# The forget gate's sigmoid written as exponential, addition and reciprocal

## The chip, the cores and the metric

One core of a Trainium2 chip runs the whole program. The metric is device time in microseconds; lower is better. A core has five engines with queues of their own: PE (TensorE, matmuls), DVE (VectorE), ACT (ScalarE, tables of functions), POOL (GpSimd) and SP (here it issues the transfers). Each queue is worked off in order, and the queues meet at semaphores only.

## What is computed

One layer of a hybrid encoder on 1024 positions of 1024 channels: four token mixers (gated recurrence, pooling, sparse attention with a top-k, attention into memory), gates, an output projection and a SwiGLU feed-forward part. The change lies in the gated recurrence (HGRN2), in four heads of 128 channels:

```python
sg = jax.nn.sigmoid(f_logit.astype(F32))
f = lbf + (1.0 - lbf) * sg
log_f = jnp.log(jnp.maximum(f, LOG_FLOOR))
k = (1.0 - lbf) * (1.0 - sg)
...
b = jnp.cumsum(lfc, axis=1)
o_inter = jnp.einsum('bthk,bhkv->bthv', qc * jnp.exp(b), S)
...
att = jnp.einsum('bthk,bshk,btshk->bhts', qc, kc, decay)
```

The sparse attention that runs beside it finds the 256th largest score of each row and masks the keys below it:

```python
top_val, top_idx = lax.top_k(score, n_sel)
```

## The kernel before

Everything is computed in transposed form, channels on the 128 partitions, in two halves of 512 positions. Each fp32 operand of a matmul is split into a high part (ACT copies it, rounded) and a low part (DVE subtracts), and a product takes three matmuls: lines 302 to 304 for a unit, where a unit is a block of 128 columns of weights times 8 blocks of channels. `Unit.split` (L283, L284) writes the tiles `wh` and `wl`, of which there are three each, and `run` splits three units ahead. The result of a unit lies in PSUM (`psB`, two buffers) until its `evac` has read it.

Beside this main line run generators, one step or so per unit: `hgrn_gen` (the recurrence of one head), `topk_gen` (a search for the threshold, bit by bit, ACT counts at L704 and DVE decides at L757 and L759; `finish`, L706 to L730, then builds the mask `bias`, of which POOL does the last step at L727 and which goes through DRAM as `bid`), `dsa_gen` (attention: scores plus bias on DVE at L804, Exp on ACT at L811 to `P`, transposes on PE at L821, copy to `PT`, product with the values at L828) and `mem_gen`. Up to the feed-forward part, a planner fills each engine's queue from the order in which the program writes the work and from when it expects operands to be ready, so neighbours in a queue need not be neighbours in the program.

The forget gate of one head and one half is `ev_hf` (L930 to L944). It reads the logits from PSUM (`p`) and works in slots of the tile `hw` (128x8x512): slot 0 is `k`, slot 4 `sg` (later f), slot 5 `fb` (later a scaled copy of f for the logarithm). Sigmoid on ACT at L934, then six TENSOR_SCALARs on DVE, L936 to L942. The unit of the query follows (`ev_hq`, a Tanh at L175), then `hgrn_gen`: two Ln on ACT (L959, L960), their sum (L961), a cumulative sum (L964), seven levels of differences, exponentials and products (L978 to L986) and small gram products on PE (L997, L1015, L1033). Slots 4 to 6 of `hw` serve as work space there; the last reader of slot 5 is L1027. `ev_hf` is called eight times: four heads in each half.

Of the kernel before, what the change touches and what calls it, by code (L numbers as in the profile page):

```python
# [15 lines left out]
AF = mybir.ActivationFunctionType  # L16
OP = mybir.AluOpType
# [19 lines left out]
def tile_hybrid_block(ctx, tc, x, x_t, mem_t, cols, w_in, w_gate, w_branch, w_out, hgrn_norm,  # L37
                      pool_w, w_mem_kv, norm_mix_post, norm_ffn_pre, norm_ffn_post,
                      w_ffn_gate_up, w_ffn_down, out):
    nc = tc.nc  # L40
# [203 lines left out]
    def need(e):  # L244
        if e in side:
            for _ in e[0]:
                pass
            side.remove(e)
# [681 lines left out]
    def ev_hf(h, hd):  # L930
        def f(p):
            need(S.get(("hgrn", h, hd - 1)))
            k, sg, fb = S["hw"][:, 0, :], S["hw"][:, 4, :], S["hw"][:, 5, :]
            nc.scalar.activation(sg, p, AF.Sigmoid)  # L934
            lb, om = lbt[:, hd, 0:1], lbt[:, hd, 1:2]
            nc.vector.tensor_scalar(k, sg, -1.0, 1.0, op0=OP.mult, op1=OP.add)  # L936
            nc.vector.tensor_scalar(k, k, om, 0.5, op0=OP.mult, op1=OP.mult)
            nc.vector.tensor_scalar(sg, sg, om, lb, op0=OP.mult, op1=OP.add)
            big = 2.0 ** 40
            nc.vector.tensor_scalar(fb, sg, big, float(np.float32(1e-30)) * big, op0=OP.mult, op1=OP.max)  # L940
            nc.vector.tensor_scalar(fb, fb, 1.0, None, op0=OP.min)
            nc.vector.tensor_scalar(sg, sg, 1.0 / big, None, op0=OP.max)  # L942
            S["hf"] = (sg, fb)
        return f  # L944
# [723 lines left out]
```

## Time and profile before

| | us |
|---|---|
| median of 3 runs | 1768.8 (1763.12 to 1772.54) |
| the profiled execution, its own time | 1767.2 |
| its span, first to last instruction | 1765.5 |
| PE busy | 1709.4 |
| DVE busy | 1199.8 |
| ACT busy | 896.5 |
| mean granted clock of TensorE | 0.985 |

PE is busy nearly all the time, and its busy time counts matmuls in flight. So an engine's own total says little; the question is at which places PE had to wait, and for whom. The profile names for each idle stretch the instruction that ended it, the releaser. The granted clock is given as a share of the full 2.4 GHz.

### The profile page before, as it was taken

What the parts mean: (1) busy time and instruction counts of PE and PEld (TensorE: products, weight loads), DVE (VectorE), ACT (ScalarE), POOL (GpSimd) and SP (SyncE); (2) the same over time, 40 slices, a digit from 0 to 9 for tenths busy, and PEclk for the clock granted to TensorE, in tenths of its full rate; (3) what the DMA queues carried; (4) which work ended last, traced back from release to release, by engine and by line L of the source; (5) the groups of instructions that cost most, each with busy time, mean ns of one, the idle gap of its engine ahead of it and who ended that gap; (6) DMA issues with size and microseconds to landing.
All of it is one profiled execution on the core that took longest, in us unless ns stands there. A gap on an engine that the chain in (4) does not pass through costs nothing.

```text
span 1765.5 us, 26374 instructions
## 1 busy us (share of the span) xinstructions
PE 1709.4 (97%) x9776; PEld 1421.4 (81%) x9776; DVE 1199.8 (68%) x2459; ACT 896.5 (51%) x1623; POOL 237.4 (13%) x261
## 2 busy tenths in 40 slices
PE   6999989999999999999999998899999999999997
PEld 5888867888887877888788887788888888888886
DVE  6587898777696579678666558687777777532533
ACT  5469867757656768776443343333223323422421
POOL 1020000000000010000000001332332231221321
PEclk8999999999999999999999999999999999999999
DMA  6756232222333573223242243323222321743534
GB/s 176 205 181 173 57 131 82 76 85 70 108 108 111 199 239 92 68 61 91 64 144 86 85 129 122 87 87 94 80 78 83 91 78 52 277 150 124 173 114 167
DMA packets 231296, 206.46 MB, mean 117 GB/s; under 512 B 16896, under 2 KB 194176, under 8 KB 230784
## 3 DMA queue, kind: packets, MB, share of 16 engines
q1 hardware_dynamic: 231168, 204.78, 37.5%
q8 instruction: 77, 1.26, 0.3%
q14 instruction: 51, 0.42, 0.1%
HBM read 167.26 MB, written 33.29 MB: 114 GB/s over the span
## 4 chain that ended last, share of the span: by engine, by line
PE 77%; DVE 11%; ACT 5%; DMA 3%; issue 3%; POOL 1%; SPq 0%; DVEq 0%; ACTq 0%; POOLq 0%
PE psB L302 8%; PE psB L304 8%; PE psB L303 8%; PE psA L1326 5%; PE psA L1327 5%; PE psA L1325 4%; PE psB L1325 2%; PE psB L1327 2%; PE psB L1326 2%; PE psA L1472 2%; PE psA L1471 2%; PE psA L1470 2%; DVE wl L284 2%; ACT cjunk L704 2%; PE psC L303 2%
## 5 line engine op out<-in xcount | busy, mean ns | idle before, releaser
L302 PE MATMUL psB<-uTh,wh 128*128 128x512 f32 x800 | 322.1, 403 | 1.5 <-ACT sig L1148 1.0
L304 PE MATMUL psB<-uTh,wl 128*128 128x512 f32 x800 | 315.4, 394 | 0.5 <-DVE wl L284 0.5
L303 PE MATMUL psB<-uTl,wh 128*128 128x512 f32 x800 | 315.6, 395 | 0.0
L284 DVE TENSOR_TENSOR wl<-raw,wh 128x1024 fp32r<-128x1024 f32 (+3 forms) x138 | 157.1, 1141 | 119.7 <-ACT wh L283 119.2
L283 ACT ACTIVATE wh<-raw 128x1024 fp32r<-128x1024 f32 (+3 forms) x138 | 136.0, 989 | 147.7 <-PE psB L303 112.1
L304 PEld LDWEIGHTS psB<-uTh,wl 128*128 128x128 f32 x800 | 151.7, 190 | 33.7 <-DVE wl L284 1.0
L302 PEld LDWEIGHTS psB<-uTh,wh 128*128 128x128 f32 x800 | 151.9, 190 | 33.0 <-ACT sig L1148 1.3
L303 PEld LDWEIGHTS psB<-uTl,wh 128*128 128x128 f32 x800 | 152.2, 190 | 29.8
L1220 DVE TENSOR_TENSOR hx<-hr,hx 128x1024 fp32r<-128x1024 f32 x44 | 78.1, 1810 | 95.5 <-ACT hx L167 95.4
L704 ACT ACTIVATE cjunk<-scr,cst 128x640 bf16<-128x640 f32 (+3 forms) x124 | 122.2, 985 | 40.5 <-DVE cst L759 35.4
L1342 ACT ACTIVATE th<-hid 128x512 f32<-128x512 f32 x44 | 27.8, 632 | 132.5 <-DVE hid L1217 132.5
L167 ACT ACTIVATE wh<-raw 128x1024 fp32r<-128x1024 f32 x22 | 23.3, 1060 | 116.0 <-issue 95.1
L1220 POOL TENSOR_TENSOR wl<-raw,wh 128x1024 fp32r<-128x1024 f32 x22 | 55.9, 2541 | 183.1 <-ACT wh L167 182.9
L180 POOL TENSOR_TENSOR rstd<-ms,mhalf 128x1 f32<-128x1 f32 (+2 forms) x35 | 26.9, 771 | 390.4 <-DVE ms L196 219.0
L1326 PE MATMUL psA<-xc,wcwl 128*128 128x512 f32 x176 | 69.5, 395 | 3.6 <-DVE xc L171 3.6
L1325 PE MATMUL psA<-xc,wcwh 128*128 128x512 f32 x176 | 69.8, 396 | 0.0
L1325 PE MATMUL psA<-xc,wcwl 128*128 128x512 f32 x176 | 69.7, 396 | 0.0
L1327 PE MATMUL psA<-xc,wcwl 128*128 128x512 f32 x176 | 69.5, 395 | 0.0
L1327 PE MATMUL psA<-xc,wcwh 128*128 128x512 f32 x176 | 69.3, 393 | 0.0
L1326 PE MATMUL psA<-xc,wcwh 128*128 128x512 f32 x176 | 69.0, 392 | 0.0
L1470 PE MATMUL psA<-wh,hx 128*128 128x512 f32 x176 | 68.5, 389 | 0.0
L1472 PE MATMUL psA<-wh,hx 128*128 128x512 f32 x176 | 68.5, 389 | 0.0
(501 smaller groups left out, 4301.0 us busy)
## 6 DMA issues: line engine op xcount, KB each, us to landing
raw<-in_w_gate_dram SPq DMA_DIRECT2D x64, 512.0 KB, 3.7
hr<-hidd SPq DMA_DIRECT2D x44, 512.0 KB, 6.0
raw<-in_w_in_dram SPq DMA_DIRECT2D x36, 512.0 KB, 4.0
raw<-in_w_ffn_gate_up_dram SPq DMA_DIRECT2D x22, 512.0 KB, 4.2
rawu<-in_w_ffn_gate_up_dram SPq DMA_DIRECT2D x22, 512.0 KB, 5.4
hidd<-hid SPq DMA_DIRECT2D x44, 256.0 KB, 2.2
raw<-in_w_ffn_down_dram SPq DMA_DIRECT2D x22, 512.0 KB, 4.5
praw<-in_w_branch_dram SPq DMA_DIRECT2D x64, 128.0 KB, 3.1
```

The costliest lines, as they stand in the source:

```text
L283: nc.scalar.activation(self.hi[:, r], self.raw[:, r], AF.Copy)
L284: nc.vector.tensor_tensor(self.lo[:, r], self.raw[:, r], f32(self.hi[:, r]), op=OP.subtract)
L302: nc.tensor.matmul(p[:, ns], whi[:, k, :], xh[:, k, ns], start=(k == 0), stop=False)
L303: nc.tensor.matmul(p[:, ns], whi[:, k, :], xl[:, k, ns], start=False, stop=False)
L304: nc.tensor.matmul(p[:, ns], wlo[:, k, :], xh[:, k, ns], start=False, stop=(k == nk - 1))
L704: nc.scalar.activation(junk[:, 0:e.L], e.sc, AF.Sign, bias=bias, accum_out=e.sum)
L1220: (eng or nc.vector).tensor_tensor(o, a, b, op=OP.subtract)
L1325: nc.tensor.matmul(p, wh[:, k], xh[:, k], start=k == 0, stop=False)
L1326: nc.tensor.matmul(p, wh[:, k], xl[:, k], start=False, stop=False)
L1327: nc.tensor.matmul(p, wl[:, k], xh[:, k], start=False, stop=k == 3)
L1470: nc.tensor.matmul(acc, self.xh[:, a, ts_], self.wh[:, a], start=f, stop=False)
L1472: nc.tensor.matmul(acc, self.xl[:, a, ts_], self.wh[:, a], start=False, stop=e)
```

## The change

The Sigmoid activation becomes an Exp of the negated logits into slot 5 of `hw`, an addition of one in place, and a reciprocal from slot 5 into slot 4. The rest of `ev_hf` stays.

```diff
             k, sg, fb = S["hw"][:, 0, :], S["hw"][:, 4, :], S["hw"][:, 5, :]
-            nc.scalar.activation(sg, p, AF.Sigmoid)
+            nc.scalar.activation(fb, p, AF.Exp, scale=-1.0)
+            nc.vector.tensor_scalar(fb, fb, 1.0, None, op0=OP.add)
+            nc.vector.reciprocal(sg, fb)
             lb, om = lbt[:, hd, 0:1], lbt[:, hd, 1:2]
             nc.vector.tensor_scalar(k, sg, -1.0, 1.0, op0=OP.mult, op1=OP.add)
```

## Rows read from the trace of the kernel before

**Rows 1.** The page's first part: busy us, share and instructions of each engine.

```profile
PE 1709.4 (97%) x9776; PEld 1421.4 (81%) x9776; DVE 1199.8 (68%) x2459; ACT 896.5 (51%) x1623; POOL 237.4 (13%) x261
```

**Rows 2.** Stretches: us, each engine's busy us (instructions), clock, DMA share, GB/s.

```profile
250.00:400.00 150.00, 145.95 (x1124) 121.36 (x1124) 116.36 (x333) 105.81 (x202) 7.38 (x7) 0.97 0.27 79
```

**Rows 3.** PE's waits, 250 to 1000 us (total, times, longest), and ACT's group L283.

```profile
PE psA L828 <- ACT PT L167: 3.6, 3, 2.2
PE psA L821 <- ACT P L811: 2.7, 2, 2.4
...
L283 ACT ACTIVATE wh<-raw 128x1024 fp32r<-128x1024 f32 (+3 forms) x138 | 136.0, 989 | 147.7 <-PE psB L303 112.1
```

**Rows 4.** Groups of instructions on ACT: busy us, mean ns, idle before.

```profile
L934 ACT ACT_TABLE_LOAD x8 | 10.3, 1283 | 0.1
```

**Rows 5.** Timeline of ACT, four places: start us, us, line, operation.

```profile
252.02 1.28 ACT L934 ACT_TABLE_LOAD   x1
253.32 0.60 ACT L934 ACTIVATE hw<-psB 128x512 f32<-128x512 f32 x1
...
259.69 1.28 ACT L811 ACT_TABLE_LOAD   x1 [2.04 <-DVE mx L809]
...
272.36 0.60 ACT L811 ACTIVATE P<-P,mx 128x384 f32<-128x384 f32 x1
...
274.08 0.57 ACT L1148 ACTIVATE sig<-psB 128x512 f32<-128x512 f32 x1
...
737.42 1.28 ACT L811 ACT_TABLE_LOAD   x1
```

**Rows 6.** Groups of instructions on DVE, forms apart: busy us, mean ns.

```profile
L941 DVE TENSOR_SCALAR hw<-hw 128x512 f32<-128x512 f32 x8 | 3.4, 425 | 0.1
...
L830 DVE RECIPROCAL rc<-sm 128x1 f32<-128x1 f32 x16 | 2.5, 159 | 5.4 <-ACT P L811 5.4
...
L887 DVE RECIPROCAL rcs<-sums 128x4 f32<-128x4 f32 x8 | 1.4, 173 | 2.8 <-ACT P L870 2.8
L185 DVE TENSOR_SCALAR ms<-hss 128x4 f32<-128x4 f32 x8 | 1.3, 165 | 0.1
...
L185 DVE TENSOR_SCALAR ms<-ss 128x1 f32<-128x1 f32 x8 | 1.2, 150 | 2.8 <-ACT un L201 2.8
```

**Rows 7.** Timeline of DVE and PE, the first gate's first gram operands and products.

```profile
280.40 0.42 DVE L986 TENSOR_TENSOR hw<-hw 128x256 f32<-128x256 f32 x1
...
284.63 1.36 PE L997 MATMUL psA<-hw 128*32 128x32 f32 x128
```

**Rows 8.** Timeline of DVE and PE at the seventh gate and after it.

```profile
819.38 0.42 DVE L1068 TENSOR_TENSOR hw<-psA,rstd 128x256 f32<-128x256 f32 x1 [0.90 <-POOL rstd L180]
...
837.72 0.69 DVE L804 CUSTOM_DVE_ANT_0 P<-psA,bias 128x512 f32<-128x512 f32 x1 [1.26 <-DMA bias<-bid]
...
841.28 1.19 PE L821 MATMUL psA<-ident,P 128*128 128x128 f32 x8 [2.38 <-ACT P L811]
```

**Rows 9.** Timeline of POOL, DVE and PE after the first gate.

```profile
265.72 1.49 POOL L727 TENSOR_SCALAR sc<-sc 128x512 f32<-128x512 f32 x1 [8.85 <-DVE sc L726]
...
268.26 0.55 DVE L804 CUSTOM_DVE_ANT_0 P<-psA,sc 128x384 f32<-128x384 f32 x1
...
272.51 1.15 PE L821 MATMUL psA<-ident,P 128*128 128x128 f32 x6 [0.28 <-ACT P L811]
```

**Rows 10.** The fifth gate: two stretches of 10 us, and timeline of DVE and PE.

```profile
660.00:670.00 10.00, 7.73 (x33) 6.30 (x32) 9.64 (x26) 6.66 (x12) 3.02 (x1) 0.73 0.42 134
...
670.00:680.00 10.00, 10.00 (x46) 8.21 (x45) 8.63 (x16) 9.21 (x14) 0.00 (x0) 0.93 0.17 52
...
664.07 0.44 DVE L936 TENSOR_SCALAR hw<-hw 128x512 f32<-128x512 f32 x1
...
691.28 0.42 DVE L986 TENSOR_TENSOR hw<-hw 128x256 f32<-128x256 f32 x1
...
691.42 0.66 PE L997 MATMUL psA<-hw 128*32 128x32 f32 x54
```

## The prediction

> **What bounds the kernel now.** I read the page's busy lines first: PE has a matmul in flight for 97% of the span, DVE is busy 68%, ACT 51% [rows 1]. So a change on ACT and DVE moves the end only where PE waits for it, or where a wait lets the granted clock fall. Then the stretches: the forget gate runs eight times (four heads, two halves of the sequence), between 252 us and 906 us. From 250 to 400 us, where the first two of them run, PE is idle for 150.00 - 145.95 = 4.05 us while DVE stands at 116.36 of 150.00, or 78% [rows 2]. The list of PE's waits over the whole zone is short; its two largest entries, 3.6 and 2.7 us, are on work of the sparse attention (P and PT), none on the forget gate itself [rows 3]. The split of the weights has its own cover: ACT's copy to wh sat idle 147.7 us, of which 112.1 until PE had left the old buffer [rows 3], so those buffers are refilled the moment they are free, about two units of matmuls before they are read. A few us more on DVE don't reach PE by that way.
>
> What can reach PE is a chain that passes through DVE where DVE has no room. I call the eight gates 1 to 8 in order of time.
>
> **What goes: table loads on ACT.** Before each Sigmoid stands an ACT_TABLE_LOAD: eight of 1283 ns [rows 4]. Exp and Tanh don't force loads on each other (the Exp at 272.36 us and the Tanh at 274.08 us have none between them) [rows 5], so an Exp in the Sigmoid's place needs none. At gates 1, 2, 5 and 6 the next function after the Sigmoid, Tanh apart, is an Exp of the attention, which pays a load only because the Sigmoid's table came in between (four loads, the first at 259.69 us, the last at 737.42 us) [rows 5]. The loads for Ln, and those for the function after it, stay. So 12 loads go: 12 x 1.28 = 15.4 us of ACT. What are they worth? One load takes 252.02 to 253.30 us, and the ACTIVATE starts 0.02 us later [rows 5]. The Trainium skill ("ScalarE: Activation LUTs", section What ACT_TABLE_LOAD costs) puts a switch at about 2.66 us, with a drain of 1.38 us; the trace does not show that drain, and by the page the loads would come to 32 us of ACT, still off PE's path. I book 0 as the value: none of PE's waits above has a vanishing load as its last releaser. The cover is PE's own queue; without it a gate would gain at most 1.3 us. The Exp itself costs what the Sigmoid did (0.60 us), and it releases the PSUM bank up to 1.3 us earlier.
>
> One wait is new: Exp writes slot 5 of hw, which L940 on DVE wrote first before. Its last reader of the gate before is L1027, in a step that the code forces to be issued before the next gate begins (the call of need at L932), and DVE reaches it long before PE has finished the unit of the next gate. Cost 0; were it late, the copies to wh would stand behind it on ACT, and they have two units of lead.
>
> **What comes: two DVE instructions per gate.** The addition in place has the form of L941 (128x512 in SBUF, immediate operands): 425 ns [rows 6]. The reciprocal of 128x512 is nowhere in the trace; the ones there have 1 to 4 elements per partition. Lower bound: another one-source DVE pass over the same tile, 0.42 us. Upper bound from its own rows: 159 ns at one element, 173 ns at four, so 4.7 ns each, times 512, plus 0.15: 2.5 us. Plain TENSOR_SCALAR grows from 150 to 165 ns over the same step, so these rows don't settle the slope [rows 6]. I take 2.5 us, since it is worked out from the only rows of this operation, and keep 0.42 for the range. So a gate adds 0.43 + 2.5 = 2.9 us to DVE (0.85 at the lower bound), eight gates 23.4 us.
>
> The Trainium skill ("VectorE: DVE Perf Modes", section First, the fixed hardware budget) describes the reciprocal as an iterative divide with a repeat count of 8. Read as eight passes per element it would, as an estimate with that page's 0.96 GHz, give 4.3 us, and by it the sum below would be 5.4 us higher; from one to four elements it would add 25 ns where the rows add 14 ns, so the trace speaks rather against that reading.
>
> **What lies on PE's path.** Inside a gate the chain gets 2.9 us of DVE and loses 1.3 us of ACT: +1.6 us until the first gram product on PE. At gate 1 the last operand is ready at 280.40 + 0.42 = 280.82 us and PE comes at 284.63 us, 3.8 us later [rows 7]; that is the least of all gates but the fifth. So the gate's own chain costs 0 outside gate 5. What remains is what the 2.9 us push back on DVE's queue, at three places.
>
> Gate 7: the same DVE queue holds the end of the last top-k row, whose bias goes from DVE over POOL to DRAM and back; L804 waits 1.26 us for that DMA at 837.72 us, and PE waits 2.38 us for its P at 841.28 us [rows 8]. There is no slack behind DVE here. Ahead of it, among the gate's own steps, DVE has a gap of 0.90 us [rows 8] that takes up part. So 2.9 - 0.9 = +2.0 us.
>
> Gate 1: the bias of a row leaves POOL at 265.72 + 1.49 = 267.21 us and the P that needs it starts at 268.26 us, so 1.0 us is free; PE then waits for that P already, 0.28 us at 272.51 us [rows 9]. So 2.9 - 1.0 = +1.9 us.
>
> Gate 5: DVE is busy 9.64 of 10 us, and the granted clock is 0.73 there [rows 10], since PE has just waited 2.2 us for PT (the longest of [rows 3]). The gate's first DVE step, L936, only starts at 664.07 us [rows 10], behind the work on which that wait hangs; in its place the new two come too late to lengthen it. But its gram has no slack: the last operand is written from 691.28 us on and PE begins at 691.42 us [rows 10]. The gaps of DVE on the way take up some, 10 - 8.63 = 1.4 us from 670 to 680 us [rows 10]. So 2.9 - 1.4 = +1.5 us.
>
> Gates 2, 3, 4, 6 and 8: no PE wait for DVE within reach, 0. Together 2.0 + 1.9 + 1.5 = +5.4 us: the profiled execution of 1767.2 us (span 1765.5 us and 1.7 us around it) would become 1772.6 us. It lies 1.6 us under the median of 1768.8 us, so against the median the forecast is **1774 us**.
>
> **Rivals.** (a) DVE turns into the bound at gates 1, 5 and 7, slower: all three pass on the full 2.9 us (8.7 us), and one more stretch runs at a clock as in 660 to 670 us, which costs (1 - 0.73) x 10 = 2.7 us. That gives 1768.8 + 11.4 = 1780 us. It decides from the point at which the gaps that I counted (0.9, 1.0 and 1.4 us) are already spoken for, or the new pair is put ahead of the top-k work. For it: DVE is at 96% from 660 to 670 us [rows 10]. Against: a gate's steps may be queued late, as L936 was. (b) The reciprocal is a plain pass at the lower bound, 0.42 us: the pair is then 0.85 us and fits in each of the gaps; 1768.8 us, no change. For it: the plain rows grow by as much as the reciprocal's [rows 6]. (c) ACT is what PE waits for: if the loads saved shorten the longest waits for PT and P (2.2 and 2.4 us) and give back one slow-clock stretch (2.7 us), 1768.8 - 7.3 = 1761 us. Against: these waits hang on DVE and a DMA. (d) The change doesn't do what it says: the queues are filled by a planner, which may put Exp and Ln so that loads come back or other work is reordered. I see no sign in the rows; within some us of no change.
>
> **How the numbers follow.** The forecast gets 0.50, (a) 0.25, (b) 0.14, (c) 0.05, (d) 0.06. The range goes from (c), 1761, to a little over (a), 1784, since the runs before lie within 1763.12 to 1772.54 us and the pair could add a further stretch at low clock. About 0.5%, or 8.8 us, is what a measurement can tell from no change. Forecast, (b) and (d) fall within; (a) lies above; half of (c) and a small part of (d) lie below 1760. Hence faster 0.03, same 0.71, slower 0.26.
>
> **What would show it.** Right: no Sigmoid load, 12 loads fewer, an ACT total some 15 us lower; a reciprocal row of about 2.5 us and DVE up by about 23 us; the PE wait of 2.38 us at gate 7 longer by some 2 us; the end within 10 us. Wrong: a reciprocal over 3 us with several PE waits for DVE (then a), under 0.7 us (then b), or PE waits that shrink after gates 2 and 6 (then c). A changed order of work far from the gates would make the whole sum void.

## The result and the profile after

The changed kernel takes 1776.4 us (median of 7 runs, 1773.4 to 1777.5), the kernel before 1764.8 us (7 runs, 1760.9 to 1772.5). The measured ratio of the two is 1.0051, with a 95% interval of 1.0034 to 1.0067. A repeat, among the experiments below, gave 1.0063 (1.0050 to 1.0075). So the change costs some 9 to 11 us. The forecast was 1774 us within 1761 to 1784 us, from a kernel before of 1768.8 us, the median of its first three runs; so the change itself was forecast at 5.4 us. The profiled execution of after took 1777.5 us (span 1775.8 us), against 1767.2 us (span 1765.5 us) before: 10.3 us between these two traces.

The busy time of each engine, from the page of after, answers to [rows 1]:

```profile
PE 1711.4 (96%) x9776; PEld 1420.6 (80%) x9776; DVE 1225.2 (69%) x2475; ACT 875.5 (49%) x1607; POOL 236.7 (13%) x261
```

ACT has 21.0 us less than before, DVE 25.4 us more. PE has the same number of instructions; it is idle for 64.4 us instead of 56.1 us and busy for 2.0 us longer. So most of the 10 us are idle time of PE, and the rest goes with stretches at a lower clock, as at gate 5 below. Next, the groups of instructions of after, on DVE and then on ACT (busy us, mean ns, idle time before); they answer to [rows 4, 6]:

```profile
L936 DVE RECIPROCAL hw<-hw 128x512 f32<-128x512 f32 x8 | 26.8, 3348 | 0.1
L935 DVE TENSOR_SCALAR hw<-hw 128x512 f32<-128x512 f32 x8 | 3.4, 424 | 0.1
...
L962 ACT ACT_TABLE_LOAD x8 | 10.3, 1283 | 0.1
L1150 ACT ACT_TABLE_LOAD x6 | 7.7, 1283 | 0.1
L811 ACT ACT_TABLE_LOAD x3 | 3.8, 1283 | 0.1
L961 ACT ACT_TABLE_LOAD x3 | 3.8, 1283 | 0.1
L870 ACT ACT_TABLE_LOAD x2 | 2.6, 1283 | 0.0
...
```

Line numbers behind L934 are two higher than before. The reciprocal takes 3348 ns, eight times a plain pass and above the upper bound of 2.5 us. No load stands on L934 any more; 23 loads are left of 39.

Where PE waits, 245 to 1170 us of after (us in total, times, longest us); this answers to [rows 3]:

```profile
PE psC L302 <- ACT ymb L167: 6.3, 2, 4.2
PE psA L821 <- ACT P L811: 5.0, 3, 2.4
...
PE psB L302 <- DVE hw L176: 3.2, 2, 2.5
...
PE psA L828 <- ACT PT L167: 1.5, 2, 1.3
```

Two entries stand out: ymb, the operand of the pooling mixer's projection, and `hw` at L176, the Tanh step of the query. The kernel before has one wait for ymb, of 2.1 us, at another place, which stays; the one of 4.2 us is new, and so are both waits for L176 (2.53 us, and 0.62 us behind gate 7). None of them was in the forecast.

To see where the time is lost I cut each trace at PE's own marks: the score product (L802) near 248 us, then the first gram product after gates 1, 2, 3, 4, 5 and 8, then the end. Each number below is the difference of two starts on PE's timeline, in us, from one profiled execution of each kernel. What each kernel does is told with the experiments.

| kernel | to gate 1 | 1 to 2 | 2 to 3 | 3 to 4 | 4 to 5 | 5 to 8 | 8 to the end |
|---|---|---|---|---|---|---|---|
| before | 35.7 | 59.4 | 87.6 | 65.6 | 194.2 | 238.2 | 835.9 |
| after | 37.4 | 59.7 | 88.9 | 65.6 | 199.2 | 239.9 | 837.2 |
| after, again | 36.2 | 59.7 | 90.5 | 65.5 | 199.2 | 240.4 | 838.9 |
| cheap instruction for the reciprocal | 31.6 | 59.3 | 87.5 | 65.6 | 195.5 | 237.8 | 838.3 |
| Tanh, not folded | 32.5 | 59.4 | 87.6 | 65.5 | 195.3 | 236.1 | 837.3 |
| Tanh folded in | 31.4 | 59.4 | 87.3 | 65.5 | 195.3 | 238.9 | 837.5 |
| half a reciprocal | 34.7 | 59.3 | 89.0 | 65.5 | 197.6 | 237.2 | 839.0 |
| reciprocal in four pieces | 37.2 | 59.4 | 87.6 | 65.5 | 199.3 | 238.1 | 837.6 |
| reciprocal twice | 40.4 | 59.7 | 87.9 | 65.6 | 206.0 | 238.5 | 836.6 |
| Sigmoid kept, reciprocal behind it | 38.8 | 59.3 | 92.8 | 65.5 | 200.8 | 240.1 | 837.4 |
| new form at gates 1 to 4 | 37.2 | 59.7 | 88.9 | 65.6 | 195.3 | 235.3 | 836.5 |
| new form at gate 5 alone | 35.5 | 59.3 | 87.3 | 65.6 | 199.1 | 239.6 | 838.0 |
| new form at gates 6 to 8 | 35.5 | 59.3 | 87.7 | 65.6 | 195.2 | 240.3 | 837.3 |
| new form but at gate 5 | 37.4 | 59.7 | 89.0 | 65.5 | 195.3 | 240.7 | 837.6 |

Between before and after: +1.7 at gate 1, +0.3, +1.3 at gate 3, 0, +5.0 at gate 5, +1.7 from 5 to 8 and +1.3 behind, together 11.3 us; after reaches the first mark 1.0 us earlier (247.98 against 248.95 us), so 10.3 us remain, as between the spans. The start of the first mark differs by up to 6 us between these executions (244.8 to 251.1 us), and the last column scatters from 835.9 to 839.0 us without a pattern; neither is read as an effect. A difference of 1 us in one row is not read either, unless other rows repeat it: after and its repeat are the same kernel, with DVE's steps in the same order, and differ by 1.2 us up to gate 1 and by 1.6 us from gate 2 to 3. Beside the kernel before (194.2 us from gate 4 to 5), six other kernels without a reciprocal at gate 5 take 195.2 to 195.5 us there, so that of the +5.0 us some 3.7 to 4.0 us are left against those.

**Gate 5, the largest part.** The timeline of after, DVE, then ACT, then PE (start us, us, engine, line; in brackets the idle time before and its releaser):

```profile
668.66 3.34 DVE L936 RECIPROCAL hw<-hw 128x512 f32<-128x512 f32 x1
...
672.38 0.22 DVE L759 SCALAR_TENSOR_TENSOR cst<-cst,cbits 128x1 int32<-128x1 int32 x1
...
675.79 0.75 DVE L1131 TENSOR_SCALAR ypb<-psA,colt 128x512 f32<-128x512 f32 x1
...
672.69 1.15 ACT L704 ACTIVATE cjunk<-scr,cst 128x1024 bf16<-128x1024 f32 x1 [4.19 <-DVE cst L759]
...
673.84 1.04 ACT L283 ACTIVATE wh<-raw 128x1024 fp32r<-128x1024 f32 x1
674.90 1.28 ACT L962 ACT_TABLE_LOAD   x1
...
676.73 0.62 ACT L167 ACTIVATE ymb<-ypb 128x512 fp32r<-128x512 f32 x1
...
677.39 0.80 PE L302 MATMUL psC<-ymb,pjw 128*128 128x512 f32 x1 [4.24 <-ACT ymb L167]
```

Read it from the end. PE stands 4.24 us at the head of its queue for ymb. ACT writes ymb at 676.73 us, from ypb, which DVE writes at 675.79 us. DVE comes to it late: the reciprocal holds it from 668.66 to 672.00 us, and 16 steps of the gate itself, the search and the sparse attention stand between it and ypb. ACT too stands still, 4.19 us, for the threshold's next step (L759 at 672.38 us), so its own queue, with the weights' copy and the Ln's load ahead of ymb, starts late. The same place in the kernel before, DVE, ACT and PE:

```profile
670.10 0.75 DVE L1129 TENSOR_SCALAR ypb<-psA,colt 128x512 f32<-128x512 f32 x1 [0.33 <-PE psA L1127]
...
673.24 0.61 ACT L167 ACTIVATE ymb<-ypb 128x512 fp32r<-128x512 f32 x1
...
664.59 2.80 PE L828 MATMUL psA<-svt,PT 128*128 128x64 f32 x12 [2.23 <-ACT PT L167]
```

There DVE still waited for PE before ypb, and PE did not wait for ymb. Its 2.23 us for PT are gone in after, which waits 1.66 us for P instead, ahead of the reciprocal, at 663.05 us. Between the marks of gates 4 and 5 PE is idle for 194.2 - 189.3 = 4.9 us before and for 199.2 - 189.0 = 10.2 us after; that is all of the +5.0. Two stretches of after show it (us, busy us of PE, PEld, DVE, ACT, POOL, granted clock, DMA share, GB/s), beside [rows 10]:

```profile
670.00:680.00 10.00, 4.75 (x17) 3.11 (x17) 10.00 (x25) 7.23 (x10) 0.00 (x0) 0.85 0.14 41
680.00:690.00 10.00, 9.51 (x39) 7.37 (x38) 7.93 (x18) 6.42 (x11) 0.00 (x0) 0.81 0.19 52
```

DVE is busy in the whole of the first one while PE works less than half of it; the granted clock then falls below its full level, as it did after the PT wait in the kernel before.

**Gate 1 and gate 3**, one line of before, then the timeline of after:

```profile
262.25 0.67 DVE L176 SCALAR_TENSOR_TENSOR hw<-hw,psB 128x512 f32<-128x512 f32 x1
```

```profile
258.03 3.35 DVE L936 RECIPROCAL hw<-hw 128x512 f32<-128x512 f32 x1
...
267.37 0.69 DVE L176 SCALAR_TENSOR_TENSOR hw<-hw,psB 128x512 f32<-128x512 f32 x1
...
268.11 0.79 PE L302 MATMUL psB<-uTh,wh 128*128 128x512 f32 x1 [2.53 <-DVE hw L176]
...
415.01 0.39 PE L863 MATMUL psA<-mkt,mqs 64*128 64x256 f32 x1 [1.07 <-ACT PT L167]
```

At gate 1 DVE's step L176 is the last reader of a `psB` buffer. It stands behind the gate's own steps and ran at 262.25 us before; now it runs at 267.37 us, and the unit that needs the buffer waits 2.53 us (3.56 us in the repeat).

### The profile page after: what moved, and what is told of

It reads as the page before. It is cut to its first block, busy times and chain, and to the rows that moved or that the text cites. A ratio compares the mean times of both kernels' runs of the same rounds, so it can differ in the third digit from the quotient of the medians.

```text
span 1775.8 us, 26367 instructions
## 1 busy us (share of the span) xinstructions
PE 1711.4 (96%) x9776; PEld 1420.6 (80%) x9776; DVE 1225.2 (69%) x2475; ACT 875.5 (49%) x1607; POOL 236.7 (13%) x261
## 4 chain that ended last, share of the span: by engine, by line
PE 52%; DVE 5%; ACT 2%; DMA 1%; issue 1%; POOL 1%; DVEq 0%; POOLq 0%; SPq 0%; ACTq 0%
PE psA L1328 5%; PE psA L1329 5%; PE psA L1327 4%; PE psB L302 3%; PE psB L304 3%; PE psB L303 3%; PE psB L1327 2%; PE psB L1329 2%; PE psB L1328 2%; PE psA L1473 2%; PE psA L1472 2%; PE psA L1474 2%; PE psC L1329 1%; PE psC L1328 1%; PE psC L1327 1%; PE psC L1473 1%
## 5 line engine op out<-in xcount | busy, mean ns | idle before, releaser
L283 ACT ACTIVATE wh<-raw 128x1024 fp32r<-128x1024 f32 (+3 forms) x138 | 136.1, 990 | 173.8 <-PE psB L303 134.8
L1222 POOL TENSOR_TENSOR wl<-raw,wh 128x1024 fp32r<-128x1024 f32 x22 | 56.1, 2551 | 182.9 <-ACT wh L167 182.7
```

The source lines that it names most:

```text
L283: nc.scalar.activation(self.hi[:, r], self.raw[:, r], AF.Copy)
L1222: (eng or nc.vector).tensor_tensor(o, a, b, op=OP.subtract)
```

## The experiments

**The theory** after the result: the cost is DVE's, the 3.35 us of one reciprocal at the head of a queue that serves other engines. **The rivals**: the planner's other order of work (rival B in the expectations where it is named), and the loads, which might be worth something after all. All edits are against the changed kernel unless said; ratios are against the kernel before, on the same chip.

**A cheap instruction in the reciprocal's place.**

```diff
-            nc.vector.reciprocal(sg, fb)
+            nc.vector.tensor_scalar(sg, fb, 0.25, 1.0, op0=OP.mult, op1=OP.min)
```

> Exp and addition as in the changed kernel, but in the reciprocal's place one TENSOR_SCALAR of the same tile (times 0.25, at most 1), so the division is left out. Theory A (the 3.35 us of each reciprocal at the head of DVE's queue is the loss): DVE falls by about 8 x 2.9 = 23 us, the PE waits of 4.24 us (gate 5) and 2.53 us (gate 1) go, ratio to the kernel before 0.998 to 1.001. Rival B (the planner's other order of work is the loss, whatever the new instructions last): ratio still about 1.005. Rival C (the loads saved on ACT are worth time by themselves): ratio under 0.997, since some 20 us of table loads are gone at nearly no price on DVE.

Measured: 1766.6 us against 1766.5 us, ratio 1.0002 (0.9991 to 1.0012). The page of this kernel:

```profile
PE 1707.0 (97%) x9776; PEld 1416.7 (80%) x9776; DVE 1202.9 (68%) x2475; ACT 880.9 (50%) x1611; POOL 237.0 (13%) x261
```

27 loads are left, exactly 12 fewer than before, and ACT has 15.6 us less. With the same number of new steps, the same Exp and the same new wait, nothing is lost. Is the other order of the work the cause, then? The planner makes another order of this kernel than of after in many places (27 loads against 23). But around the two gates where after waits most, DVE's queue holds the same steps in the same order in both: from 246 to 276 us of after, at gate 1, and from 507 to 701 us, at gate 5; ACT has one step at another place in each. Gate 5 with the cheap instruction, on DVE:

```profile
664.40 0.41 DVE L936 TENSOR_SCALAR hw<-hw 128x512 f32<-128x512 f32 x1
...
665.20 0.21 DVE L759 SCALAR_TENSOR_TENSOR cst<-cst,cbits 128x1 int32<-128x1 int32 x1
...
668.60 0.75 DVE L1131 TENSOR_SCALAR ypb<-psA,colt 128x512 f32<-128x512 f32 x1
```

The step at L936 takes 0.41 us instead of 3.34 us, ypb starts 4.2 us behind it instead of 7.1 us, and PE's wait for ymb is 1.14 us instead of 4.24 us; the wait at gate 1 is 0.78 us instead of 2.53 us (lines further below). At these two gates the order is thus not the cause. At the other gates it differs, and this run does not tell the two apart. Nothing is gained in the total by the loads either. At gate 1 they are worth something, though: 31.6 us instead of 35.7 up to its gram. PE's waits of the kernel before for sig (1.0 us) and for P ([rows 9]) are not there, and its granted clock from 270 to 280 us is 1.00 instead of 0.83. The kernels with Tanh have 31.4 and 32.5 us, those with a Sigmoid at gate 1 35.5 to 35.7 us. Whether it is the loads themselves or the order that comes with their absence was not told apart. Where these 3 to 4 us go in the total is not settled: it is not in one later stretch.

**The Sigmoid kept, with the addition and the reciprocal behind it.**

```diff
-            nc.scalar.activation(fb, p, AF.Exp, scale=-1.0)
+            nc.scalar.activation(fb, p, AF.Sigmoid)
```

> Sigmoid kept on ACT with its table loads, but written where the Exp writes and followed by the same addition and reciprocal (so the gate's value is 1/(1+sigmoid), not the reference's). Theory A: the DVE part is the loss and the loads are worth nothing, so the ratio stays at 1.004 to 1.007. Rival C: the loads saved gave back part of it, so without that saving the ratio goes to 1.008 or more (20 us of ACT more, of which a third would reach PE).

Measured: 1780.4 us, ratio 1.0081 (1.0067 to 1.0095), above both ratios of after and where rival C was expected. So beside the reciprocal the loads seem to cost 0.2 to 0.3% (3 to 5 us), though without it their absence shows no gain in the total; against the repeat of after the two intervals overlap. PE's waits of this kernel from 245 to 1000 us, then a wait at gate 3:

```profile
PE psA L821 <- ACT P L811: 10.8, 3, 6.3
...
414.28 0.38 PE L863 MATMUL psA<-mkt,mqs 64*128 64x256 f32 x1 [1.81 <-ACT PT L167]
```

At gate 5 PE now waits 6.3 us for P instead of 4.2 us for ymb. The stretch from gate 2 to 3 takes 92.8 us (88.9 and 90.5 in after), that from 4 to 5 200.8 us (199.2 in both).

**Sigmoid by Tanh, without a reciprocal** (against the kernel before).

```diff
-            nc.scalar.activation(sg, p, AF.Sigmoid)
+            nc.scalar.activation(sg, p, AF.Tanh, scale=0.5)
+            nc.vector.tensor_scalar(sg, sg, 0.5, 0.5, op0=OP.mult, op1=OP.add)
```

> Only the half of the change that removes the table loads: the sigmoid as 0.5 tanh(x/2) + 0.5, Tanh on ACT in place of Exp, and one TENSOR_SCALAR on DVE in place of addition and reciprocal. Theory A: DVE gets 8 x 0.42 = 3.4 us, ACT loses some 15 to 20 us of loads; nothing of this lies on PE's path, ratio 0.998 to 1.001. Rival B: any new instruction reorders the work, ratio anywhere from 0.995 to 1.006 without a cause in the gate. Rival C: 0.997 or less.

Measured: 1763.7 us, ratio 0.9989 (0.9977 to 1.0002), 27 loads, DVE 1200.7 us. Not told apart from the kernel before.

**The reciprocal in four pieces.**

```diff
-            nc.vector.reciprocal(sg, fb)
+            for c in range(4):
+                s = slice(c * 128, (c + 1) * 128)
+                nc.vector.reciprocal(sg[:, s], fb[:, s])
```

> The changed kernel with the reciprocal cut into four instructions of 128 columns, so that other work of DVE can go between them; DVE's total is the same or some 0.4 us per gate more. Theory A in its strict form (the block of 3.35 us at the queue's head is what hurts, not the total): the ratio falls to 1.000 to 1.003. If the total of DVE's work near the gates is what hurts: ratio stays at 1.004 to 1.007. Four instructions of about 0.9 us each are expected.

Measured: 1772.3 us, ratio 1.0034 (1.0021 to 1.0046). The reciprocal's line in this kernel (ns least, median, largest; first and last start), then PE's waits:

```profile
L938 DVE RECIPROCAL hw<-hw x32: 892/896/955, 254.9 to 911.0; 128x128 f32<-128x128 f32 x32
...
PE psC L302 <- ACT ymb L167: 6.3, 2, 4.2
```

The total on DVE is no smaller (4 x 896 = 3584 ns), the wait for ymb is the same 4.2 us and from gate 4 to 5 it takes 199.3 us. What came back is at gate 3 (87.6 us instead of 88.9 and 90.5) and from 5 to 8 (238.1 instead of 239.9 and 240.4). But it did not come back because other steps went in between: at gates 3, 4, 5, 6 and 8 the four pieces follow each other without a gap, and only at gates 1, 2 and 7 do other steps stand among them. Two whole reciprocals give nearly the same two rows (87.9 and 238.5 us, below). So this run does not test whether the block or the total hurts, and its ratio, which lies between the two expectations and overlaps that of after, stays unexplained.

**Half of the reciprocal** (the other 256 columns get a cheap instruction).

```diff
-            nc.vector.reciprocal(sg, fb)
+            nc.vector.reciprocal(sg[:, 0:256], fb[:, 0:256])
+            nc.vector.tensor_scalar(sg[:, 256:512], fb[:, 256:512], 0.25, 1.0, op0=OP.mult, op1=OP.min)
```

> The changed kernel with a reciprocal of 256 columns and a TENSOR_SCALAR on the other 256 (there the division is left out). The reciprocal should last 1.7 to 1.8 us. Theory A: half the dose, ratio 1.001 to 1.003, under half of the whole one's 1.0051 if gaps of DVE take up the first microsecond. A threshold only (nothing until the gaps are full): 1.000.

**The reciprocal twice** (the second one's result is not read).

```diff
             nc.vector.reciprocal(sg, fb)
+            nc.vector.reciprocal(fb, fb)
```

> The changed kernel with a second reciprocal behind the first at every gate (on the slot that is overwritten later; the result is the reference's). DVE gets 8 x 3.35 = 26.8 us more. Theory A (DVE's queue near the gates, with part of each 3.35 us passed on to PE): the second dose costs more than the first, since the gaps are used up: ratio 1.010 to 1.016. If the planner hides what it knows of: 1.005 to 1.008.

Measured: half of it takes 1750 ns and gives 1770.1 us, ratio 1.0032 (1.0016 to 1.0047); two give 1783.7 us, ratio 1.0100 (1.0085 to 1.0115). PE's waits at gate 1 and gate 5, first with the cheap instruction alone, then half, then twice (one fence for each kernel):

```profile
268.30 0.50 PE L302 MATMUL psB<-uTh,wh 128*128 128x512 f32 x1 [0.78 <-DVE hw L176]
...
670.06 0.73 PE L302 MATMUL psC<-ymb,pjw 128*128 128x512 f32 x2 [1.14 <-ACT ymb L167]
```

```profile
264.76 0.50 PE L302 MATMUL psB<-uTh,wh 128*128 128x512 f32 x1 [2.32 <-DVE hw L176]
...
671.76 0.72 PE L302 MATMUL psC<-ymb,pjw 128*128 128x512 f32 x2 [3.38 <-ACT ymb L167]
```

```profile
268.11 0.79 PE L302 MATMUL psB<-uTh,wh 128*128 128x512 f32 x1 [5.95 <-DVE hw L176]
...
683.01 0.80 PE L302 MATMUL psC<-ymb,pjw 128*128 128x512 f32 x1 [7.27 <-ACT ymb L167]
```

And the stretch of the last kernel in which its longest wait ends (columns as above):

```profile
680.00:690.00 10.00, 6.13 (x16) 4.56 (x17) 8.14 (x20) 7.60 (x10) 0.00 (x0) 0.50 0.17 52
```

With 0, 256, 512 and twice 512 columns of reciprocal at each gate the wait at gate 5 is 1.14, 3.38, 4.24 (4.22 in the repeat) and 7.27 us, the one at gate 1 0.78, 2.32, 2.53 (3.56) and 5.95 us, and the ratio 1.0002, 1.0032, 1.0051 to 1.0063, and 1.0100. Up to gate 1's gram it takes 31.6, 34.7, 36.2 to 37.4, and 40.4 us, from gate 4 to 5 195.5, 197.6, 199.2 and 206.0 us. From one reciprocal to two the wait at gate 5 grows by 3.03 us and the one at gate 1 by 2.4 to 3.4 us, nearly its whole 3.35 us. Of the 6.8 us at gate 5, 3.0 us are idle time of PE and 3.9 us longer busy time (192.9 against 189.0 us), which goes with the clock: in the last line it is 0.50, the lower of its two levels (1.2 GHz) for the whole stretch. Two of the expectations failed: half the columns cost half of the loss or more, not less, and the second reciprocal adds 0.0037 to 0.0049, no more than the first. No size shows below which the reciprocal would be free.

**Which gates.** `ev_hf` with the new form at some gates and the Sigmoid at the others:

```diff
-            nc.scalar.activation(fb, p, AF.Exp, scale=-1.0)
-            nc.vector.tensor_scalar(fb, fb, 1.0, None, op0=OP.add)
-            nc.vector.reciprocal(sg, fb)
+            if (h, hd) == (1, 0):
+                nc.scalar.activation(sg, p, AF.Sigmoid)
+            else:
+                nc.scalar.activation(fb, p, AF.Exp, scale=-1.0)
+                nc.vector.tensor_scalar(fb, fb, 1.0, None, op0=OP.add)
+                nc.vector.reciprocal(sg, fb)
```

This one keeps the Sigmoid at gate 5. The others turn the condition round (new form at gate 5 alone), or use `h == 0` (new form at gates 1 to 4) or `h == 1 and hd > 0` (gates 6 to 8) for the new form.

> The changed kernel, but the fifth gate alone keeps its Sigmoid. By the traces the distance between the two kernels grows by 6 us of 9 around the fifth gate, where DVE has no gap. If that is so, this gives back 4 to 7 us: ratio 1.001 to 1.003. If the loss belongs to all gates alike (1.1 us each): 1.0045. If the planner's order moves the loss elsewhere: 1.004 or more with the wait of 4.24 us at another place.

> The new form at gate 5 alone, Sigmoid at the other seven. If the block of 3.35 us in DVE's full queue at gate 5 is the main place: a PE wait for ymb of about 4 us there, ratio 1.002 to 1.004. If a single gate is never worth more than its share: 1.0006, not to be told from 1.

> The new form at gates 1 to 4 (first half of the sequence), Sigmoid at the others. By the traces the changed kernel is 2.4 us behind when gate 5 begins, of which 1.7 us from gate 1. If the loss sits where the traces show it: ratio 1.001 to 1.002. If it belongs to all gates alike: 1.0025 to 1.003.

> The new form at gates 6 to 8, Sigmoid at the others. By the traces the distance grows by some 1 to 2 us from gate 6 to the end, and gate 7, where 2.0 us was forecast, shows none: ratio 1.000 to 1.001. If the forecast for gate 7 holds after all: 1.001 to 1.002. If all gates are alike: 1.002.

> The changed kernel once more, unedited, on the chip and beside the runs of the three kernels below, so that the parts can be set against the whole. Ratio 1.0034 to 1.0067, as before.

| new form at gates | us | ratio | 95% |
|---|---|---|---|
| 1 to 4 | 1767.4 | 1.0000 | 0.9988 to 1.0013 |
| 5 | 1772.7 | 1.0031 | 1.0020 to 1.0042 |
| 6 to 8 | 1768.2 | 1.0005 | 0.9994 to 1.0016 |
| all but 5 | 1774.2 | 1.0046 | 1.0034 to 1.0059 |
| all (after, again) | 1778.9 | 1.0063 | 1.0050 to 1.0075 |

PE's wait at gate 5 in the kernel that has the new form there alone:

```profile
672.24 0.79 PE L302 MATMUL psC<-ymb,pjw 128*128 128x512 f32 x1 [4.20 <-ACT ymb L167]
```

Gate 5 alone makes the ymb wait of after, the stretch of 199.1 us, and, on its own, about half of the loss (0.0031 of 0.0051 to 0.0063). In the kernel without it there the ymb wait is absent and PE's 2.1 us for PT are back. But taken out of the eight it gives back only 0.0005 to 0.0017, where 1.001 to 1.003 was expected for the rest. The parts don't add up: 0.0000 + 0.0031 + 0.0005 = 0.0036 against 0.0063 (each with an interval of about 0.0012 to either side, so this difference is barely clear of noise), and all gates but 5 cost 0.0046 where the two groups alone give 0.0005 (this one is clear of it). The table of marks shows where: with the new form at gates 1 to 4 the loss there is the full 1.5 + 0.3 + 1.3 us, and the stretch from 5 to 8, which has the Sigmoid as before, is 2.9 us shorter (235.3 against 238.2). With one plain reciprocal at gates 6 to 8 that stretch takes 239.9 to 240.7 us, without one 235.3 to 239.6 us, and with two 238.5 us; so no price of these three gates can be read from it. The planner makes another order out of each kernel; which step of that order saves the 2.9 us was not found, and why they are not there in the kernel with all gates stays open.

**Tanh with its halves folded into the constants**, so that nothing is added on DVE (against the kernel before).

```diff
-    lbt = st([128, 4, 2], name="lbt")
+    lbt = st([128, 4, 4], name="lbt")
...
+        nc.vector.tensor_scalar(lbt[:, :, 2], lbt[:, :, 1], 0.5, None, op0=OP.mult)
+        nc.vector.tensor_tensor(lbt[:, :, 3], lbt[:, :, 0], lbt[:, :, 2], op=OP.add)
...
-            nc.scalar.activation(sg, p, AF.Sigmoid)
-            lb, om = lbt[:, hd, 0:1], lbt[:, hd, 1:2]
+            nc.scalar.activation(sg, p, AF.Tanh, scale=0.5)
+            omh, lbh = lbt[:, hd, 2:3], lbt[:, hd, 3:4]
...
-            nc.vector.tensor_scalar(k, k, om, 0.5, op0=OP.mult, op1=OP.mult)
-            nc.vector.tensor_scalar(sg, sg, om, lb, op0=OP.mult, op1=OP.add)
+            nc.vector.tensor_scalar(k, k, omh, 0.5, op0=OP.mult, op1=OP.mult)
+            nc.vector.tensor_scalar(sg, sg, omh, lbh, op0=OP.mult, op1=OP.add)
```

> The sigmoid by Tanh with its halves folded into the constants of the steps that follow (f = t (1-lb)/2 + lb + (1-lb)/2), so that no instruction is added to a gate and the Sigmoid's table loads go. Theory A: PE waits for none of this, ratio 0.997 to 1.000, not to be told from the Tanh version's 0.9989. Were ACT's loads on PE's path: 0.996 or less.

Measured: 1764.6 us against 1765.6 us, ratio 0.9992 (0.9980 to 1.0003). With the other Tanh and the cheap instruction there are thus three kernels without the Sigmoid's loads and without a reciprocal, all within 0.15% of the kernel before. Both Tanh kernels beat after; neither can be told from before.

## Why the prediction came out as it did

The time was within the range and 2.4 us above the forecast (4.9 us in the repeat), but the way there was right in part only. That it came so near is in part luck: the forecast started from 1768.8 us, where seven runs of the kernel before have their median at 1764.8 us. The change itself was forecast at 5.4 us and is 9 to 11 us, nearly twice as much.

- **The loads are worth 0 on the path: right in the total, wrong at gate 1.** The three kernels without a reciprocal show no gain that can be measured. But all three are 3 to 4 us quicker up to the first gram, against a forecast of at most 1.3 us for a gate without cover, so that the change's +1.7 us there (+0.5 in the repeat) are some 5 to 6 us of the reciprocal less about 4 of what goes with the missing loads. And with the reciprocal in place the loads seem to be worth 3 to 5 us.
- **12 loads, 15.4 us: right in the plain case** (12 fewer and 15.6 us with the cheap instruction; 12 fewer with Tanh). In after 16 went and ACT fell by 21.0 us: the four at L175 and the one at L981 are gone as well, the two Ln lines have 11 instead of 13, L811 3 instead of 6, and L870 has two new ones. ACT's queue was put in another order, which is rival (d) in small; a price of its own could not be shown.
- **The addition, 425 ns: right** (424 ns).
- **The reciprocal, 2.5 us: wrong.** It takes 3.35 us; both bounds lay below. The step that failed is the line through the rows of one and four elements: 4.7 ns an element there, but (3348 - 896) / 384 = 6.4 ns from 128 to 512 columns. A slope from a difference of 14 ns is no bound. The pair so costs 3.35 + 0.42 = 3.8 us a gate, not 2.9, and eight gates 30 us of instructions, not 23.4; DVE's busy total rose by 25.4 us. The Trainium skill ("VectorE: DVE Perf Modes", section First, the fixed hardware budget) gives a repeat count of 8; the prediction read it as 4.3 us, and judged that the rows spoke against it. The measured 6.4 ns are, as an estimate with that page's 0.96 GHz, some 6.1 clocks a column: between the forecast's 4.5 (4.7 ns) and eight; by that reading of the page the sum would have been 1779 us.
- **Gate 7, +2.0 us: wrong.** PE's wait for P there is the same 2.38 us as in [rows 8], 2.85 us in the repeat, and 2.31 us with two reciprocals. The delay on DVE did come. Two lines of before, then four of after:

```profile
817.54 0.42 DVE L936 TENSOR_SCALAR hw<-hw 128x512 f32<-128x512 f32 x1
...
826.64 1.28 DVE L726 SCALAR_TENSOR_TENSOR scr<-scr,cst,tkg 128x1024 f32<-128x1024 f32 x1
```

```profile
826.97 0.42 DVE L935 TENSOR_SCALAR hw<-hw 128x512 f32<-128x512 f32 x1
...
828.93 3.34 DVE L936 RECIPROCAL hw<-hw 128x512 f32<-128x512 f32 x1
...
850.90 0.69 DVE L804 CUSTOM_DVE_ANT_0 P<-psA,bias 128x512 f32<-128x512 f32 x1 [1.98 <-DMA bias<-bid]
...
854.80 0.47 PE L821 MATMUL psA<-ident,P 128*128 128x128 f32 x1 [2.38 <-ACT P L811]
```

  From the gate's first step on DVE to L804 it is 23.9 us in after and 20.2 us in before ([rows 8]), 3.8 us more. But PE's queue changed too. From the gram of gate 6 to this wait (columns as above, before and after):

```profile
778.62:841.28 62.66, 60.28 (x505) 50.51 (x505) 52.49 (x137) 38.92 (x61) 4.25 (x3) 1.00 0.29 86
788.01:854.80 66.79, 63.44 (x517) 52.80 (x516) 55.59 (x139) 35.35 (x59) 4.03 (x3) 1.00 0.27 80
```

  In after PE has 12 matmuls more ahead of the wait and is busy 3.2 us longer, so P comes later and PE comes later for it. The step that failed is to have held PE's queue as it was while DVE's moved. The stretch from gate 5 to 8 grew by 1.7 us (2.1 with the new form at gates 6 to 8 alone), but kernels without a reciprocal there differ by 4.3 us among themselves, so this is not shown to be a price of gate 7.
- **Gate 1, +1.9 us: the size was near (+1.7, and +0.5 in the repeat) by luck, the mechanism wrong.** It is the difference of a gain and a larger loss, and not P but the reader of the `psB` buffer behind the gate's steps on DVE (L176) was late.
- **Gate 5, +1.5 us: mis-sized, +5.0 us** (3.7 us against the kernel with the cheap instruction, whose order on DVE is the same there). The forecast looked along the gate's own chain to its gram, and held the PT wait safe since L936 came late. Both hold: PT's wait even went. The step that failed is to have asked only who waits for the gate. In DVE's queue ypb stood behind the reciprocal. So did L759, the answer of the search, for which ACT waited 4.19 us with ymb further back in its own queue. The gaps counted there (1.4 us) were spoken for, which is the condition of rival (a).
- **Gates 2, 3, 4, 6 and 8, nothing: wrong at gate 3**, +1.3 us (a PE wait of 1.07 us for PT of the memory attention; +2.9 us in the repeat, but only 87.9 us in all and no such wait with two reciprocals, so it hangs on the order as well), right at 2 and 4 (+0.3 and 0); 6 and 8 were not measured apart.
- **The rivals.** (a), DVE as the bound with 1780 us, comes nearest in kind: a reciprocal over 3 us and new PE waits that come from DVE were its signs, and both are there. Its price per gate was too high at 7 and too low at 5, and the repeat (1778.9 us) lies between it and the forecast. (b) falls with 3.35 us. (c) may have seen rightly that ACT's loads hold PE, at gate 1, but in the total the three kernels without a reciprocal show nothing of its 7 us. Of (d), the order of the work did change, but with the cheap instruction, where it changed too, the time did not.

The sum was thus made of errors that went against each other: too little for the instruction and for gate 5, 2.0 us at a wait that did not move, and a base 4 us too high. What is shown is that the reciprocal's time on DVE is the cause (no loss without it, more with more of it, and at gates 1 and 5 with the same order on DVE) and that gate 5 on its own costs about half, through ymb. What stays open is the price of each of the other gates: it depends on which order the planner makes of them all.

## What to carry to other kernels

To see who pays for a long instruction on an in-order engine, list what stands behind it in that engine's queue and who waits for each of these, other generators included; the chain of the changed work itself was the least of it here. A saving spread over an engine off the path (some 16 us of ACT) showed nothing in the total, and a cost on an engine that others wait for (25 us of DVE, in pieces of 3.35) showed by a third or more. To be rid of Sigmoid's loads, a function that shares its neighbours' table (Tanh, with its halves folded into constants) costs nothing that could be measured, where a reciprocal costs 3.35 us for each 128x512 tile.

## What the runs showed of the hardware

- The reciprocal on DVE takes 896, 1750 and 3348 ns for 128, 256 and 512 fp32 columns in SBUF, about 6.4 ns a column, while a plain TENSOR_SCALAR takes 424 ns for 512. Rows of one to four elements (159 to 173 ns, [rows 6]) show almost nothing of it.
- In the stretch of 10 us in which a wait of PE of 7.27 us ended, the granted clock was 0.50; with a wait of 4.24 us it was 0.85 in the stretch with the wait and 0.81 in the next.
- Tanh and Exp have no load between them in these traces, except where a Sigmoid stood just ahead of the Tanh (one place in before, at 259.69 us). A Sigmoid by Tanh has 27 loads in the whole kernel instead of 39, or 31 with its halves folded in; there all but the first stand between Ln and one of the two.
